# Splitting a strided transpose of a 90-degree rotation over VectorE and ScalarE, with all transfers on one queue

## The chip, the cores and the metric

The kernel runs on one core of a Trainium2 chip. The metric is the time of one execution in microseconds (us), as the median of several runs. The profiled span is about 1.77 us shorter than the timed value (122.9 against 124.67 for the kernel before), because a part of each execution lies outside the span.

## The reference

Each of 96 images (32 x 3) of 256 x 256 floats is rotated clockwise by 90 degrees. Nothing is computed; 25.17 MB are read and 25.17 MB are written.

```python
batch, c, h, w = 32, 3, 256, 256
x = np.random.randn(batch, c, h, w).astype(np.float32)
def reference(x):
    return np.rot90(x, k=-1, axes=(-2, -1)).astype(np.float32)
```

## The kernel before

A slab is 128 partitions of 8 image rows each, so four images and 1 MB; there are 24 slabs. 32 partitions hold one image. VectorE transposes blocks of 32 x 32, and the access patterns around the transpose do the rest. Reading, it steps through a row 8 floats (32 bytes) apart; writing, it steps backwards, 32 bytes apart as well. Each slab takes two transposes of 128x1024. Loads are issued on SP, stores on ScalarE's queue.

```python
R = 8; G = H // R; n_slabs = B * C * G // P   # 8, 32, 24
PARTS = 2; CP = R // PARTS
in_pool  = ctx.enter_context(tc.tile_pool(name="in_pool",  bufs=12))
out_pool = ctx.enter_context(tc.tile_pool(name="out_pool", bufs=12))
for n in range(n_slabs):
    t_in = in_pool.tile([P, R * W], fp32, tag="t_in")
    nc.sync.dma_start(out=t_in, in_=ld_v[n])
    t_out = out_pool.tile([P, R * W], fp32, tag="t_out")
    src = t_in.rearrange("p (r g c) -> p c r g", r=R, c=R)
    dst = t_out.rearrange("p (c g r) -> p c r g", c=R, r=R)[:, :, ::-1, ::-1]
    for k in range(PARTS):
        cs = slice(k * CP, (k + 1) * CP)
        nc.vector.transpose(out=dst[:, cs], in_=src[:, cs])
    nc.scalar.dma_start(out=st_v[n], in_=t_out)
# ... cut: the launch
```

## Time and profile before

| | before |
|---|---|
| time, median | 124.7 us (124.66 to 124.83) |
| span | 122.9 us |
| bytes moved | 50.34 MB, mean 410 GB/s |
| VectorE busy | 94.6 us (77%), 2.05 us for one transpose |

The following lines are from the profile's page of the kernel before. First come the engines' busy times; then the mean busy share of the DMA engines in 40 equal slices of the span, in tenths, and under it the GB/s in each slice; then the queues, the chain of waits, the costliest group, and the issues of transfers with the median us from issue to landing.

```profile
DVE 94.6 (77%) x48; POOL 0.2 (0%) x4
...
DMA  2999999999999999999999999999999999999994
GB/s 93 427 427 403 339 424 427 427 429 427 427 432 427 427 427 427 432 429 427 427 427 427 429 427 427 427 427 429 427 427 427 427 429 427 427 429 427 427 424 171
...
q1 hardware_dynamic: 3456, 25.17, 49.2%
q10 hardware_dynamic: 3456, 25.17, 48.5%
...
DMA t_in<-in_x_dram 89%; DVE t_out L51 2%; DVEq L79 2%; SPq L44 1%; DVEq L51 0%
...
L51 DVE STREAM_TRANSPOSE t_out<-t_in 128x1024 f32<-128x1024 f32 x48 | 94.6, 2052 | 20.9 <-DMA t_in<-in_x_dram 15.4
```

The reader should see that the DMA row stays at 9 from the second slice to the second last, and that nearly every slice runs at 427 GB/s. 50.34 MB at 427 GB/s is 117.9 us of the 122.9. The chain of waits agrees, with 89% in loads. VectorE is at 77%; it waits for loads and not the other way round.

The missing 5.0 us lie at three places: the start (the first slice has 93 GB/s), the end (the last has 171), and a dip in the fifth slice. The windows of one microsecond show the dip; the columns are the stretch, its length, the busy us of VectorE and of GpSimd with the number of instructions, the granted clock, the DMA share, and the GB/s.

```profile
10.00:11.00 1.00, 1.00 (x1) 0.00 (x0) 1.00 1.07 451
11.00:12.00 1.00, 1.00 (x2) 0.00 (x0) 1.00 0.94 360
12.00:13.00 1.00, 1.00 (x1) 0.00 (x0) 1.00 1.06 311
13.00:14.00 1.00, 1.00 (x2) 0.00 (x0) 1.00 0.96 287
14.00:15.00 1.00, 1.00 (x1) 0.00 (x0) 1.00 0.94 393
15.00:16.00 1.00, 1.00 (x2) 0.00 (x0) 1.00 0.99 418
```

Between 11 and 15 us the DMA engines count as busy, yet move less. Against 427 GB/s the four lines lack 357, so about 0.84 us of transfer are lost. The first store was issued at 9.67 us.

### The profile page before, as it was taken

To read this page: it belongs to the slowest core of one execution; us is meant where nothing else is said; L and a number is where in the kernel's file an instruction comes from. 1 tells how busy PE (TensorE), PEld (TensorE's weight loads), DVE (VectorE), ACT (ScalarE), POOL (GpSimd) and SP (SyncE) were. 2 spreads that over 40 slices of the span, in tenths; PEclk is the share of its full clock that TensorE was granted. 3 is DMA by queue.
4 is the path that set the end of the run, shared out by engine and by line. 5 is a ranking of instruction groups with operands and counts; after the bars stand their busy time and mean duration, and the time that the engine had idled before them with its cause. 6 is when DMAs were issued, how large, how long until landed. Compare 5 with 4: busy or idle time off the path is not lost.

```text
span 122.9 us, 186 instructions
## 1 busy us (share of the span) xinstructions
DVE 94.6 (77%) x48; POOL 0.2 (0%) x4
## 2 busy tenths in 40 slices
DVE  0199999999897697796977967979769779797500
POOL 0000000000000000000000000000000000000000
DMA  2999999999999999999999999999999999999994
GB/s 93 427 427 403 339 424 427 427 429 427 427 432 427 427 427 427 432 429 427 427 427 427 429 427 427 427 427 429 427 427 427 427 429 427 427 429 427 427 424 171
DMA packets 6913, 50.34 MB, mean 410 GB/s; under 512 B 768, under 2 KB 768, under 8 KB 768
## 3 DMA queue, kind: packets, MB, share of 16 engines
q1 hardware_dynamic: 3456, 25.17, 49.2%
q10 hardware_dynamic: 3456, 25.17, 48.5%
q14 instruction: 1, 0.01, 0.0%
HBM read 25.17 MB, written 25.17 MB: 410 GB/s over the span
## 4 chain that ended last, share of the span: by engine, by line
DMA 89%; DVE 2%; DVEq 2%; SPq 1%; issue 0%
DMA t_in<-in_x_dram 89%; DVE t_out L51 2%; DVEq L79 2%; SPq L44 1%; DVEq L51 0%
## 5 line engine op out<-in xcount | busy, mean ns | idle before, releaser
L51 DVE STREAM_TRANSPOSE t_out<-t_in 128x1024 f32<-128x1024 f32 x48 | 94.6, 2052 | 20.9 <-DMA t_in<-in_x_dram 15.4
L68 POOL MEMSET const-uint8-127<- 128x1 uint8 x1 | 0.1, 102 | 0.0
L68 POOL MEMSET const-bfloat16-1.0<- 128x1 bf16 x1 | 0.1, 101 | 0.0
L68 POOL MEMSET const-float32-0.0<- 128x1 f32 x1 | 0.1, 98 | 0.2 <-issue 0.2
L68 POOL MEMSET const-float32-1.0<- 128x1 f32 x1 | 0.1, 98 | 0.0
## 6 DMA issues: line engine op xcount, KB each, us to landing
t_in<-in_x_dram SPq DMA_DIRECT2D x24, 1024.0 KB, 19.6
out_dram<-t_out ACTq DMA_DIRECT2D x24, 1024.0 KB, 16.5
```

The costliest lines, as they stand in the source:

```text
L44: nc.sync.dma_start(out=t_in, in_=ld_v[n])
L51: nc.vector.transpose(out=dst[:, cs], in_=src[:, cs])
L68: nc = _bacc.Bacc("TRN2", target_bir_lowering=False, num_devices=1)
L79: with _tile.TileContext(nc) as tc:
```

## The change

VectorE now writes its transposed blocks contiguously into a middle tile. ScalarE copies from there into the output rows: it reads 128 bytes apart, backwards, and writes contiguously. All transfers go on SP's queue, since ScalarE is to be free for copying, and nine loads are issued ahead, so that a store that waits for its data does not hold back loads behind it. The intent is to take strided writing off VectorE and share the work.

```diff
-    in_pool = ctx.enter_context(tc.tile_pool(name="in_pool", bufs=12))
-    out_pool = ctx.enter_context(tc.tile_pool(name="out_pool", bufs=12))
+    in_pool = ctx.enter_context(tc.tile_pool(name="in_pool", bufs=11))
+    mid_pool = ctx.enter_context(tc.tile_pool(name="mid_pool", bufs=4))
+    out_pool = ctx.enter_context(tc.tile_pool(name="out_pool", bufs=11))
+    ins = []
+    def load(n):
+        t_in = in_pool.tile([P, R * W], fp32, tag="t_in")
+        nc.sync.dma_start(out=t_in, in_=ld_v[n])
+        ins.append(t_in)
+    for n in range(AHEAD):      # AHEAD = 9
+        load(n)
     for n in range(n_slabs):
-        t_in = in_pool.tile([P, R * W], fp32, tag="t_in")
-        nc.sync.dma_start(out=t_in, in_=ld_v[n])
         t_out = out_pool.tile([P, R * W], fp32, tag="t_out")
-        src = t_in.rearrange("p (r g c) -> p c r g", r=R, c=R)
-        dst = t_out.rearrange("p (c g r) -> p c r g", c=R, r=R)[:, :, ::-1, ::-1]
+        src = ins[n].rearrange("p (r g c) -> p c r g", r=R, c=R)
+        dst = t_out.rearrange("p (c g r) -> p c g r", c=R, r=R)
         for k in range(PARTS):
             cs = slice(k * CP, (k + 1) * CP)
-            nc.vector.transpose(out=dst[:, cs], in_=src[:, cs])
-        nc.scalar.dma_start(out=st_v[n], in_=t_out)
+            t_mid = mid_pool.tile([P, CP, R, G], fp32, tag="t_mid")
+            nc.vector.transpose(out=t_mid, in_=src[:, cs])
+            nc.scalar.copy(
+                out=dst[:, cs],
+                in_=t_mid.rearrange("p c r g -> p c g r")[:, :, ::-1, ::-1],
+            )
+        nc.sync.dma_start(out=st_v[n], in_=t_out)
+        if n + AHEAD < n_slabs:
+            load(n + AHEAD)
```

More of the change, by code (lines that the diff above doesn't have):

```diff
@@ L34 @@
     CP = R // PARTS
+    AHEAD = 9
     ld_v = x.rearrange("b c h w -> (b c h) w").rearrange("(n p r) w -> n p (r w)", p=P, r=R)
     st_v = out.rearrange("b c h w -> (b c h) w").rearrange("(n p c) w -> n p (c w)", p=P, c=R)
-    in_pool = ctx.enter_context(tc.tile_pool(name="in_pool", bufs=12))
-    out_pool = ctx.enter_context(tc.tile_pool(name="out_pool", bufs=12))
-    for n in range(n_slabs):
+    in_pool = ctx.enter_context(tc.tile_pool(name="in_pool", bufs=11))
[3 more added lines that the diff above has]
+    def load(n):
         t_in = in_pool.tile([P, R * W], fp32, tag="t_in")
         nc.sync.dma_start(out=t_in, in_=ld_v[n])
+        ins.append(t_in)
+    for n in range(AHEAD):
+        load(n)
+    for n in range(n_slabs):
         t_out = out_pool.tile([P, R * W], fp32, tag="t_out")
-        src = t_in.rearrange("p (r g c) -> p c r g", r=R, c=R)
-        dst = t_out.rearrange("p (c g r) -> p c r g", c=R, r=R)[:, :, ::-1, ::-1]
+        src = ins[n].rearrange("p (r g c) -> p c r g", r=R, c=R)
+        dst = t_out.rearrange("p (c g r) -> p c g r", c=R, r=R)
         for k in range(PARTS):
             cs = slice(k * CP, (k + 1) * CP)
-            nc.vector.transpose(out=dst[:, cs], in_=src[:, cs])
-        nc.scalar.dma_start(out=st_v[n], in_=t_out)
+            t_mid = mid_pool.tile([P, CP, R, G], fp32, tag="t_mid")
[7 more added lines that the diff above has]
+            load(n + AHEAD)
 _INS = ['x']
```

## The prediction

> **What bounds the kernel now.** The span is 122.9 us (124.67 timed, so 1.77 us lie outside it). The 40-slice strip shows DMA at 9 in every slice but the first and last, GB/s near 427; the chain of waits is 89% DMA of t_in; VectorE is busy 94.6 us (77%). Data movement is the limit: 50.34 MB at 427 GB/s is 117.9 us. The other 5.0 us, from strip and one-microsecond windows: about 2.4 us before the DMA engines run, about 0.8 us in a dip at 11 to 14.5 us (down to 287 GB/s, DMA share still near 1), when the first stores join the loads, and about 1.8 us after the last packet. The Trainium skill, "DMA: Bandwidth & Descriptors", section "Where 436 GB/s comes from", puts the ceiling at 435 GB/s; 427 agrees.
>
> **What the change does.**
> - VectorE: the same 48 transposes of 128x1024, now with contiguous output: 2.04 us each today (the t_out group), 1.1 to 2.05 us expected.
> - ScalarE: 48 new copies of 128x1024. No trace has one. An estimate from the Trainium skill, "ScalarE: Activation LUTs", section "What ACT_TABLE_LOAD costs" (186 ns + 0.833 ns per element) is 1.04 us; with a penalty for reading 128 bytes apart, perhaps 2 us.
> - One slab of load and store takes 2 x 1.05 MB / 427 GB/s = 4.91 us of DMA, so each engine may spend 2.45 us per half slab. Both stay below it, in parallel, off the critical path.
> - Transfers: same bytes, same 8 KB packets, one queue instead of two, loads running ahead. Each transfer still waits for the one eight before it, so up to eight (about 20 us of work) are outstanding. In before, loads alone on one queue (start) and stores alone (end) both run near 427 GB/s, so one queue in order should fill the engines. The first store is issued at about 11 to 12 us, behind some four loads; later SP should always find its tile ready.
> - The end: nine stores remain after the last load, so the last transpose and copy hide behind about 17 us of queued stores. But before has no starvation there (424 GB/s in the slice before last), so nothing is won.
>
> **Net.** The 117.9 us of transfer and 4.2 us of start and end stay. Only the 0.8 us dip may go, or move to about 25 us, when the first store comes up behind the loads. Against it stands a small possible cost where one queue switches from read to write. I predict 124.3 us, 8 in 10 within 123.4 to 126.0. Faster by over 2%: 0.02; within 2%: 0.93; slower by over 2%: 0.05.
>
> **What would show each step.** Right: the strip stays near 427 GB/s, one queue holds about 97% of the DMA time, VectorE and ScalarE under 90% busy, a copy under 2.45 us, the chain of waits mostly DMA, median issue to landing near 20 us for loads and stores alike. If the dip follows the second queue's first use, it vanishes and the span is about 122.1; if it follows the first writes to memory, it moves.
>
> **What would make it wrong.** A ScalarE copy over 2.45 us: then 48 copies set the time; 2.7 us each gives about 137 us. SP blocking in order on a store that waits for ScalarE: GB/s would sag in the middle. A bubble at each switch between load and store in one ring: 48 of 0.05 us would cost 2.4 us.

## The result, and the profile after

The changed kernel takes 124.98 us (median, 124.95 to 125.19) against 124.72 us. The ratio is 1.0024, with a 95% interval from 1.0006 to 1.0041: the same, a quarter of a microsecond slower. Ratios here are the mean time of one kernel's fast runs over that of the other's in the same rounds, so they are not quite the ratio of the medians quoted.

These are the lines of the changed kernel's page that answer to those above, with ScalarE's own.

```profile
DVE 93.8 (76%) x48; ACT 94.6 (77%) x49; POOL 0.2 (0%) x4
...
DMA  4999999999999999999999999999999999999994
GB/s 93 420 426 428 426 426 423 359 370 426 426 426 434 428 428 434 426 426 426 426 428 426 428 428 426 428 426 426 426 426 426 420 426 426 434 426 431 426 428 170
...
q1 hardware_dynamic: 6912, 50.33, 98.0%
...
DMA t_in<-in_x_dram 78%; ACT t_out L64 3%; SPq L50 2%; DVE t_mid L63 2%; DVEq L63 0%
...
L63 DVE STREAM_TRANSPOSE t_mid<-t_in 128x1024 f32<-128x1024 f32 x48 | 93.8, 2010 | 10.6 <-DMA t_in<-in_x_dram 10.6
L64 ACT COPY t_out<-t_mid 128x1024 f32<-128x1024 f32 x48 | 93.3, 2008 | 11.0 <-DVE t_mid L63 11.0
L64 ACT ACT_TABLE_LOAD x1 | 1.3, 1283 | 0.7 <-PEq L85 0.7
...
t_in<-in_x_dram SPq DMA_DIRECT2D x24, 1024.0 KB, 19.6
out_dram<-t_out SPq DMA_DIRECT2D x24, 1024.0 KB, 19.6
```

The strip of GB/s is what it was, and the single queue carries 98% of the DMA time. The transpose hardly became faster by writing contiguously: 2.01 us, where it was 2.05 (experiment 11 returns to this). ScalarE now does as much work as VectorE, 2.01 us for each copy. Both have slack, and the span is 123.2 us. The dip is still there, but in the eighth and ninth slice. The windows of the changed kernel show where (now with a column for ScalarE after VectorE's):

```profile
22.00:23.00 1.00, 1.00 (x1) 1.00 (x1) 0.00 (x0) 1.00 0.99 410
23.00:24.00 1.00, 1.00 (x2) 1.00 (x2) 0.00 (x0) 1.00 1.21 393
24.00:25.00 1.00, 1.00 (x1) 1.00 (x1) 0.00 (x0) 1.00 0.91 221
25.00:26.00 1.00, 1.00 (x2) 1.00 (x2) 0.00 (x0) 1.00 0.93 344
26.00:27.00 1.00, 1.00 (x1) 1.00 (x1) 0.00 (x0) 1.00 1.01 426
```

Between 23 and 26 us 323 of 3 x 427 are missing, about 0.76 us. The first store was issued at 11.71 us, but it stood in line behind the nine loads issued before it. At 427 GB/s these take about 22 us (an estimate, 9 x 1.05 MB / 427 GB/s), and with the 2.4 us before the engines run, its turn comes at about 24 us; the dip waited for that. So the dip goes with the turn of the first store in its queue, not with its issue, and not with the first use of a second queue.

Where compute ends tells the same story as the chain. Before, the last transpose ended at 115.4 us, 7.5 us before the end of the span. After, the last copy ended at 106.3 us, 16.9 us before it: more slack at the end, which wins nothing, since stores fill that stretch at 427 GB/s either way.

### The profile page after: what moved, and what is told of

It reads as the page before. It is cut to its first block, busy times and chain, and to the rows that moved or that the text cites. A ratio compares the mean times of both kernels' runs of the same rounds, so it can differ in the third digit from the quotient of the medians.

```text
span 123.2 us, 262 instructions
## 1 busy us (share of the span) xinstructions
DVE 93.8 (76%) x48; ACT 94.6 (77%) x49; POOL 0.2 (0%) x4
## 4 chain that ended last, share of the span: by engine, by line
DMA 78%; ACT 3%; SPq 2%; DVE 2%; issue 1%; DVEq 0%
DMA t_in<-in_x_dram 78%; ACT t_out L64 3%; SPq L50 2%; DVE t_mid L63 2%; DVEq L63 0%
## 5 line engine op out<-in xcount | busy, mean ns | idle before, releaser
L63 DVE STREAM_TRANSPOSE t_mid<-t_in 128x1024 f32<-128x1024 f32 x48 | 93.8, 2010 | 10.6 <-DMA t_in<-in_x_dram 10.6
L64 ACT COPY t_out<-t_mid 128x1024 f32<-128x1024 f32 x48 | 93.3, 2008 | 11.0 <-DVE t_mid L63 11.0
L64 ACT ACT_TABLE_LOAD x1 | 1.3, 1283 | 0.7 <-PEq L85 0.7
## 6 DMA issues: line engine op xcount, KB each, us to landing
t_in<-in_x_dram SPq DMA_DIRECT2D x24, 1024.0 KB, 19.6
out_dram<-t_out SPq DMA_DIRECT2D x24, 1024.0 KB, 19.6
```

Source lines behind the costliest of these rows:

```text
L63: nc.vector.transpose(out=t_mid, in_=src[:, cs])
L64: nc.scalar.copy(out=dst[:, cs], in_=t_mid.rearrange("p c r g -> p c g r")[:, :, ::-1, ::-1],)
```

## The experiments

My theory was that transfers bound both kernels, that the new compute is off the critical path as long as each engine stays within a budget per half slab, and that only the dip could be won. Twelve kernels tested it.

### 1 and 2: each half of the change alone

Transfers alone: one queue and nine loads ahead, with VectorE writing the output rows as in the kernel before.

```diff
-            t_mid = mid_pool.tile([P, CP, R, G], fp32, tag="t_mid")
-            nc.vector.transpose(out=t_mid, in_=src[:, cs])
-            nc.scalar.copy(...)
+            nc.vector.transpose(out=dst[:, cs], in_=src[:, cs])   # dst as in the kernel before
```

> The transfers part of the change alone: one queue, nine loads ahead, VectorE writing the output rows itself, no ScalarE copy. My theory: the +0.26 us of the changed kernel is a matter of the transfers (loads alone in a deep queue ran at 424.5 GB/s between 11 and 22 us, against 428 in the mixed stretch), so this kernel should take 124.8 to 125.1 us, like the changed kernel, with the dip near 24 us. Rival: the 0.26 us comes from the new ScalarE copy and its longer path; then this kernel takes 124.6 to 124.75 us, like the kernel before.

Measured: 125.12 us, ratio 1.0032 (1.0019 to 1.0044), 0.02 us above the range expected. Without any ScalarE copy the small loss is there in full, so it belongs to the transfers part of the change (queue, order of issue, or eleven buffers in place of twelve; no run separates these). The dip lies between 23 and 26 us, as in the changed kernel. Where the 0.3 us are lost is not settled: the mean rate of the first 11 us is 332 GB/s here and 334 in the kernel before, which would be 0.05 us, and the rest is spread too thin to name.

Compute alone: middle tile and ScalarE copy, but loads on SP and stores on ScalarE's queue as in the kernel before.

```diff
-            nc.vector.transpose(out=dst[:, cs], in_=src[:, cs])
+            t_mid = mid_pool.tile([P, CP, R, G], fp32, tag="t_mid")
+            nc.vector.transpose(out=t_mid, in_=src[:, cs])
+            nc.scalar.copy(out=dst[:, cs], in_=...)               # as in the change
         nc.scalar.dma_start(out=st_v[n], in_=t_out)               # stays on ScalarE
```

> The compute part alone: middle tile and ScalarE copy, but loads on SP and stores on the ScalarE queue, in the order of the kernel before. If compute is off the critical path, 124.6 to 125.0 us with the dip back near 12 to 15 us, and ScalarE's busy time near 95 us. Rival: ScalarE, which now also waits to issue stores, holds back its own copies, the first stores come late and the time rises by over 1 us.

Measured: 126.74 us, ratio 1.0163 (1.0149 to 1.0177), so the rival won and my theory missed (the ratio is within 2%, but its interval is clear of 1). The waits of this kernel (engine, its instruction, the one waited for: us in total, times, longest) and its strip of GB/s show why; the last three lines are from its order in time, where the columns are start, length, engine, and instruction, with the idle time before it.

```profile
ACT t_out L54 <- DMA t_in<-in_x_dram: 15.9, 2, 12.4
```

```profile
GB/s 94 427 432 422 361 387 432 419 419 427 445 427 419 419 432 440 427 419 419 437 437 424 419 422 432 442 421 419 424 432 437 421 416 424 437 432 393 251 283 220
```

```profile
58.94 1.95 ACT L54 COPY t_out<-t_mid 128x1024 f32<-128x1024 f32 x1
...
72.90 0.34 ACTq L59 DMA_DIRECT2D out_dram<-t_out  x1
73.28 3.83 ACT L54 COPY t_out<-t_mid 128x1024 f32<-128x1024 f32 x2 [12.39 <-DMA t_in<-in_x_dram]
```

ScalarE took its instructions in order here. At 60.9 us its next instruction was a store that had to wait for an earlier transfer, and ScalarE stood still for 12.39 us, though the transposes for the two copies behind that store had ended at 64.53 us. The transfers ran on at full rate for a while on what was buffered, so nothing showed. But from 90 us on ScalarE copied without a pause, at about 3.8 us per slab, and after the last load its copies alone set the pace of the stores: the last slices fall to 251, 283 and 220 GB/s. The 2 us are thus ScalarE's lost time, presented at the end. This reading rests on the trace; no run takes away that one wait alone. But the changed kernel differs from this one only in queue and order of its transfers, so it is the move to SP, with its lookahead, that kept the new copies from costing 2 us.

### 3 and 4: can the dip be taken away?

If the dip were a one-time cost of the first writes to memory, a small store at the very start, before the loads run at full rate, should pay it for nothing.

```diff
+    warm = warm_pool.tile([P, 128], fp32, tag="warm")
+    nc.vector.memset(warm, 0.0)
+    nc.scalar.dma_start(out=st_v[0][:, 0:128], in_=warm)   # nc.sync in the changed kernel
```

> The kernel before, plus one small early store (128 rows of 512 B of zeros into the first output slab, overwritten later). Theory: the dip of about 0.8 us is a one-time cost of the first writes to memory, so an early small write takes it away while the engines are still idle: time 123.8 to 124.2 us, no stretch under 400 GB/s at 11 to 15 us. Rival: the dip is the filling of the store pipeline (store packets in flight before any completes), which each first real store pays: time unchanged or up by the added transfer, 124.7 to 124.9, dip still there.

> The changed kernel, plus the same small early store. Same theory: the dip near 24 us goes and the time falls by about 0.8 us to 124.0 to 124.4 us. Rival: dip stays near 24 us and the time is 124.9 to 125.2.

Measured: 124.78 us on the kernel before (ratio 1.0003, 0.9991 to 1.0016) and 125.06 us on the changed one (1.0023, 1.0009 to 1.0036). Neither gained, so the theory falls as stated. The strips, the kernel before with the early store first and then the changed kernel with it:

```profile
GB/s 80 421 426 400 349 426 426 429 429 426 426 429 429 432 429 426 432 429 426 426 426 426 426 426 426 426 426 429 426 429 432 426 426 429 426 426 426 421 429 187
```

```profile
GB/s 74 420 425 428 425 425 425 396 412 425 428 425 428 425 425 425 428 422 425 425 428 430 433 428 425 425 438 428 430 422 425 420 425 425 425 425 425 425 436 122
```

On the kernel before the dip remains almost whole (349 GB/s in the fifth slice, where it was 339). On the changed kernel it is shallower (396 and 412 in place of 359 and 370): in one-microsecond windows from 22 to 27 us, 0.45 us of transfer are missing, where the changed kernel misses 0.80. But the first slice lost (74 in place of 93), and so did the last (122 in place of 170), and the time did not follow. Each kernel was profiled in one execution, so half a dip gone is not certain; if it is real, a cost that every first full store pays whole does not fit it either. What the dip is stays open. The runs show only that it comes once in each kernel whose transfers otherwise run at full rate, about when the first full store has its turn, and that it costs about 0.8 us without the early store.

### 5 and 6: how much slack has ScalarE? First try

After each copy, ScalarE copies a small constant tile besides (128x128, then 128x512).

```diff
             nc.scalar.copy(out=dst[:, cs], in_=...)
+            nc.scalar.copy(out=pad_b[:, :128], in_=pad_a[:, :128])   # or 512
```

> The changed kernel with one more ScalarE copy of 128x128 after each of the 48 copies (and ten input buffers in place of eleven, for room). Estimated at about 0.3 us each, so ScalarE needs about 2.3 us per half slab, under the 2.45 us that the transfers of a half slab take. Theory (compute is off the critical path, budget 2.45 us): ScalarE busy about 110 us, time unchanged, 124.8 to 125.6 us. Rival (ScalarE is already part of what sets the time): the time rises by some 10 us, with its busy time.

> The same with an extra copy of 128x512, estimated at about 0.6 us, so about 2.6 us per half slab, over the budget of 2.45 us. Theory: ScalarE becomes the limit: about 7.7 us to its first copy, 48 x 2.62 = 126 us, and about 5 us for the last store: 136 to 142 us, GB/s sagging under 427 in the middle. Rival (a wide slack hides it): unchanged.

Measured: 124.87 us (ratio 1.0028, 1.0007 to 1.0048) and 129.94 us (1.0425, 1.0409 to 1.044). The first is as expected, the second rose, but by far less than the sum said, though the extra copies took what was estimated (298 and 618 ns). The experiment was flawed: the extra copies depend on nothing, and the scheduler put many of them early. In the first run 14 stood before the first real copy, where ScalarE would have idled; in the second 7 did, and the last 24 real copies came without any. So neither run tells the limit. The next pair ties the extra work to the data.

### 7 and 8: how far ahead must the loads be?

```diff
-    AHEAD = 9
+    AHEAD = 2        # or 4
```

> The changed kernel with two loads ahead in place of nine. Store n and load n+2 are issued when tile n is copied; the load lands some 7.4 us later (5.0 us from issue to landing unqueued, plus 2.46 us for the store in front), transposes and copies take 6.1 us, so two slabs take 13.5 us: 6.75 us per slab against the 4.91 us of their transfers. Theory: 155 to 175 us. Rival (the transfers still fill each other's gaps): under 130 us.

> The changed kernel with four loads ahead. By the same sum 13.5 us for four slabs, 3.4 us per slab, below 4.91 us, so the transfers are the limit again: 124.8 to 126.0 us. If nine loads ahead are needed for the full rate, it is over 127 us.

Measured: 166.84 us with two (ratio 1.3393, 1.3367 to 1.3419) and 125.75 us with four (1.0088, 1.0073 to 1.0104). Both lie in the expected ranges. With two ahead the transfers are no longer the limit; the chain of waits turns into a ring, of which this is one round (start, length, what):

```profile
65.56 0.33 SPq L68
...
65.95 0.02 SPq L50
...
65.99 6.93 DMA t_in<-in_x_dram
...
73.02 2.03 DVE t_mid L63
...
75.08 3.88 ACT t_out L64 x2
...
78.97 0.33 SPq L68
```

A store is issued, then the load two slabs ahead; it lands 6.93 us later; a transpose of 2.03 us and two copies of 3.88 us follow, and the next store of this ring comes 13.4 us after the first (the stores between belong to a second ring of the same kind). That is two slabs in 13.4 us, 6.7 us each, where their transfers need 4.91. Nine loads ahead are thus not what makes the changed kernel good, but in-order issue without lookahead would have made it bad by a third. Four loads nearly suffice; what they lose, 0.8 us against nine (in different rounds), shows for the most part near the start, where the stretch from 14 to 18 us averaged 283 GB/s ((238 + 213 + 369 + 311) / 4, the dip included), and the rate is full again until the last two slices.

### 9 and 10: the slack again, tied to the data

Each copy is followed by a second copy of a part of the same half slab to the same place, so it can't run before its data.

```diff
             nc.scalar.copy(out=dst[:, cs], in_=...)
+            nc.scalar.copy(out=dst[:, cs][:, 0:1, 0:16], in_=...[:, 0:1, 0:16])   # 128x128; or [:, 0:2], 128x512
```

> A cleaner repeat of the slack test: each ScalarE copy is followed by a copy of one eighth of the same half slab (128x128) to the same place, so the extra work cannot be moved ahead of the data. ScalarE needs about 1.94 us (2.008 us less the 0.07 us by which copies overlap) plus about 0.34 us, 2.28 us per half slab, under 2.45 us. Theory: unchanged, 124.8 to 125.7 us. Rival (the first slack test passed only because a third of its extra work ran early): over 127 us.

> The same with half of each half slab copied again (128x512): about 1.94 + 1.03 = 2.97 us per half slab, over 2.45 us. Theory: ScalarE sets the time, 7.7 us to its first copy, 48 x 2.97 = 142.6 us, about 5 us for the last store and 1.8 us outside the span: 152 to 160 us. Rival (other slack hides it): under 140 us.

Measured: 126.48 us with the eighth (ratio 1.0136, 1.0123 to 1.015) and 156.48 us with the half (1.2537, 1.2517 to 1.2556). The second is as summed. The first is a miss, and so is its rival's figure: under 2.45 us per half slab, and yet 1.5 us slower than the changed kernel. Its strip and the end of ScalarE's order in time:

```profile
GB/s 89 415 426 428 428 431 423 365 407 433 428 426 428 426 423 431 428 428 428 426 426 431 426 431 418 423 431 431 423 431 426 423 431 426 420 439 423 391 158 226
```

```profile
92.06 2.00 ACT L64 COPY t_out<-t_mid 128x1024 f32<-128x1024 f32 x1
...
96.77 2.00 ACT L64 COPY t_out<-t_mid 128x1024 f32<-128x1024 f32 x1
...
119.67 0.41 ACT L68 COPY t_out<-t_mid 128x128 f32<-128x128 f32 x1
```

Two copies start 4.71 us apart, with one other copy and two small ones between, so ScalarE takes 2.355 us per half slab. It starts at 7.7 us, and 48 x 2.355 = 113 us bring it to 120.7 us; the last copies are a little shorter, and the last ends at 120.08 us (119.67 + 0.41). The span ends 4.7 us after that. A steady-rate budget forgets these two ends. The whole line must fit into the span that the transfers would take: (123.2 - 7.7 - 4.7) / 48 = 2.31 us per half slab. At 2.355 the last stores wait for their copies, and the strip falls to 158 GB/s. Two things were thus wrong in what was expected: the limit, and the need, since the small copy took 408 ns and not 340. The 2.28 us expected would have passed under 2.31 as well. The 2.31 is an estimate; the runs only enclose it, with 1.94 us harmless and 2.355 us costing 1.5 us. The run with the half copy has the same ends: its last copy ends at 150.08 us, 4.7 us before the end of the span. The changed kernel itself needs about 1.94 us (93.3 us / 48), and is well inside.

### 11: what makes a transpose and a copy 2 us?

The result is wrong on purpose: both read contiguously.

```diff
-            nc.vector.transpose(out=t_mid, in_=src[:, cs])
+            nc.vector.transpose(out=t_mid, in_=<the contiguous half of t_in>)
-            nc.scalar.copy(out=dst[:, cs], in_=<t_mid, 128 bytes apart, reversed>)
+            nc.scalar.copy(out=dst[:, cs], in_=<t_mid, contiguous>)
```

> Wrong result on purpose: the transposes and the copies read their tile contiguously, with the same sizes and the same outputs. If the strided reads are what makes a transpose and a copy 2.0 us, the copy falls to about 1.04 us[...] and the transpose to about 1.1 us. If contiguous reads change nothing, both stay at 2.0 us. The time stays at 124.5 to 125.5 us either way, as the transfers set it.

One run: 125.05 us. Its output is wrong, which doesn't matter for the time. The two groups from its page:

```profile
L63 DVE STREAM_TRANSPOSE t_mid<-t_in 128x1024 f32<-128x1024 f32 x48 | 56.9, 1224 | 45.9 <-DMA t_in<-in_x_dram 45.2
L64 ACT COPY t_out<-t_mid 128x1024 f32<-128x1024 f32 x48 | 50.1, 1045 | 51.8 <-DVE t_mid L63 49.8
```

The copy falls from 2008 to 1045 ns, as expected, and the transpose from 2010 to 1224 ns, 0.1 us above what was expected. So the way they read is the cost: for the transpose the distance of 32 bytes, for the copy the distance of 128 bytes together with the reversal, which this run took away with it. For the copy the extra copies of the slack tests confirm it. The first two lines are of contiguous copies (experiments 5 and 6), the other two of copies that read like the real one (9 and 10):

```profile
L72 ACT COPY pad_b<-pad_a 128x128 f32<-128x128 f32 x48 | 14.3, 298 | 1.1
L72 ACT COPY pad_b<-pad_a 128x512 f32<-128x512 f32 x48 | 29.7, 618 | 1.0
...
L68 ACT COPY t_out<-t_mid 128x128 f32<-128x128 f32 x48 | 19.4, 408 | 1.4
L68 ACT COPY t_out<-t_mid 128x512 f32<-128x512 f32 x48 | 50.4, 1064 | 1.1
```

From 128 to 512 elements the contiguous copy grows by 320 ns, 0.83 ns for each element more, and the strided one by 656 ns, 1.71 ns. What is left without the elements is about 190 ns in both. So the strided, reversed reading about doubles the cost of an element and not the fixed part.

The change removed the strided write of the transpose and left its strided read, and that is why VectorE gained so little. Even the 2% between 2.05 and 2.01 us are not sure: the transposes that write contiguously have means of 2010 to 2047 ns in the changed kernel and experiments 2, 5 to 10, those that write strided 2041 to 2052 ns in the kernel before and experiments 1, 3 and 12. And although both engines fell to 46% and 42% busy with contiguous reads, the time did not move: the plainest evidence that compute is off the critical path.

### 12: is there something better than both?

The kernel before with transfers of two slabs (2 MB), half as many.

```diff
-    for n in range(n_slabs):
-        t_in = in_pool.tile([P, R * W], fp32, tag="t_in")
-        nc.sync.dma_start(out=t_in, in_=ld_v[n])
+    for m in range(n_slabs // 2):
+        t_in2 = in_pool.tile([P, 2, R * W], fp32, tag="t_in")      # bufs=6
+        nc.sync.dma_start(out=t_in2, in_=ld2[m])
         # ... the transposes for each of the two slabs, then one store of both
```

> The kernel before with transfers of two slabs (2 MB) in place of one, half as many of them. If each transfer has a fixed cost inside the steady stream (its 16 completion packets), [...]the time falls by 0.3 to 0.8 us. Rival: the 8 KB packets alone set the rate, and coarser tiles only add latency: 124.6 to 126 us.

Measured: 124.56 us, ratio 0.9983 (0.9971 to 0.9996): faster than the kernel before by 0.2%, and below the changed kernel's 124.98 us, though the two were not timed in the same rounds. The expected gain was over-sized. The strip:

```profile
GB/s 86 388 428 428 428 425 348 425 428 428 428 428 428 428 428 428 428 428 428 428 428 428 428 428 428 428 428 428 428 428 428 428 428 428 423 433 425 425 431 214
```

It stands at 428 for most of the span, with one dip to 348 and a slower second slice (388). With 24 transfers fewer the gain is 0.2 us, about 0.01 us for each. The fixed cost of a transfer inside a steady stream is therefore nearly nothing, and what is left above the pure transfer time is start, dip and end.

## Why the prediction was right

- **The limit.** It said that 117.9 us of transfer set the time and that the new compute would not. Shown: cutting VectorE's busy time to 56.9 us and ScalarE's to 51.4 (contiguous reads) leaves 125.05 us (one run), and leaving the ScalarE copy out leaves 125.12 us.
- **One queue would fill the DMA engines.** Shown: 98.0% on one queue, about 427 GB/s, issue to landing 19.6 us for loads and stores. The Trainium skill, "DMA: Bandwidth & Descriptors", section "Issuing engines are not separate DMA queues", says that all queues run on the same 16 engines and that a second one saves only issue time; this case agrees: one queue ran at about 427 GB/s, as two did.
- **The operations.** The transpose came at 2.01 us, inside 1.1 to 2.05 but at its dear end; the copy at 2.01 us, at the dear guess ("perhaps 2 us"). That penalty was worked out from nothing, so hitting it was luck. The contiguous copy took 1045 ns, where the formula that the prediction takes from "ScalarE: Activation LUTs" gives 1.04 us.
- **The dip.** The prediction left open whether it would vanish or move, and credited about half of it. It moved to 23 to 26 us and kept its size. This is the mis-sized term: 124.3 us supposed some 0.4 us won, and nothing was won; 0.26 us were lost instead, which lie in the transfers part of the change and are not further explained. So a small gain was forecast and a small loss came, well inside the stated range. The switch from load to store in one ring does not cost the feared 0.05 us each time: added up from the trace's packet records, between 35 and 110 us the changed kernel falls behind a stream of 427.5 GB/s by about 0.1 us, over some 30 switches, the kernel of experiment 1 with the same switches by 0.05 us or less, and the kernel before by nothing.
- **The budget of 2.45 us per half slab.** It was too wide. With the start of 7.7 us and the end of 4.7 us it is an estimated 2.31 us. It did no harm here, at 1.94 us.
- **What the prediction weighed too little.** It did not say what moving the stores to SP saves once ScalarE copies: copies on ScalarE with the stores left there cost 2 us. It named in-order issue on SP as a risk, rightly, but not how much lookahead guards against it: 166.84 us with two loads ahead, 125.75 with four.

## What to carry to other kernels

When the strip of GB/s is flat and the DMA engines are busy throughout, as here, dividing the compute among engines is unlikely to win anything; see first that it loses nothing. Look at an engine that both computes and issues transfers: here its copies stood behind a waiting store for 12.39 us, and the loss appeared much later, when the buffers had run dry. When you reckon how long an engine may take per tile, subtract the time before its first tile and after its last from the span, and only then divide.

## What the Trainium skill lacked or had wrong

- "Advanced Engine Details and Errata", section "SBUF Cachelines", says that accesses which each touch another 16-byte line pay a penalty, but gives no size; no page has one for a ScalarE copy or for VectorE's transpose, though sizes for another VectorE operation stand elsewhere in the skill. Here, for 128x1024 floats, reads 128 bytes apart and backwards made a ScalarE copy 2008 ns in place of 1045, and reads 32 bytes apart made a VectorE transpose 2010 ns in place of 1224 (the second figures from one run). A strided write on top of the strided read of the transpose added at most about 2% (2.05 us against 2.01), which the spread between runs nearly covers.
- "ScalarE: Activation LUTs", section "What ACT_TABLE_LOAD costs": the table load of 1283 ns and the 186 ns + 0.833 ns per element for a contiguous copy both agree (1283 ns, and 1045 ns for 1024 elements). The section does not warn that it holds for contiguous reads only; the strided copy took nearly twice as long.
- No page read has the dip of about 0.8 us at the turn of the first full store; an early store of 64 KB did not win it back (124.78 against 124.7 us, and 125.06 us on the changed kernel).
- "DMA: Bandwidth & Descriptors", section "Issuing engines are not separate DMA queues", calls the issuing engine a matter of issue time. It does not say what the choice can cost when the engine also computes: copies behind a waiting store stood still for 12.39 us in one piece here, and that cost 2 us of the total.
